# Even and odd columns in a triangular substitution, its reordering on ScalarE, and the first query weights of the last stage in places of their own

## The chip, the cores and the metric

One core of one Trainium2 chip runs the whole program in one launch. The metric is the time of an execution on the device, in microseconds (us); the kernel before has a median of 973.35 over three runs (969.14 to 974.21). The engines are TensorE (PE in the profile, PEld its weight loads), VectorE (DVE), ScalarE (ACT), GpSimd (POOL) and SyncE (SP), which issues the weights' DMAs.

## The reference, cut to what matters

The model has four mixers on 256 tokens of width 1,024: latent attention, block attention with a relative bias, a gated delta rule, and an attention with a forget gate ("fox"). The first two have a feed-forward layer behind each. The change touches the third mixer and the start of the fourth. In the delta rule, chunks of 64 tokens need the solution of a unit lower triangular system for each head:

```
a_mat = jnp.where(strict, einsum('bhncd,bhnsd->bhncs', kb, kc) * decay, 0.0)
rhs   = jnp.concatenate([vc * bc[..., None], kb * jnp.exp(gcum)[..., None]], axis=-1)
sol   = lax.linalg.triangular_solve(a_mat, rhs, left_side=True, lower=True, unit_diagonal=True)
...
y = gdn_mixer(rms_norm_2(h, pre), ...);  h = h + rms_norm_2(y, gdn_post_norm)
...
q, z = split(rms_norm_2(h, fox_pre_norm) @ fox_w_in);  k, v, f = split(rms_norm_2(h, kv_norm) @ kv_w)
```

All is computed in float32.

## The kernel before, in words

A weight matrix comes in pieces of 128 x 1,024 through a ring of four buffers `raw` (`load_w`, L148). ScalarE rounds a piece to `whi` (L164), a second engine computes the rest `wlo` as raw minus `whi` (L165; this is called a split here), and three matmuls (L171 to L173) make the product: high by high, low by high, and high by the low part of the other side. `whi` and `wlo` have rings of four buffers too, so a new piece waits until TensorE has used an old one. `raw` is free when its split is done, and only then does SyncE issue the next DMA. The split runs on VectorE, unless `engines` says otherwise.

The order on each engine is set by a scheduler that goes by data dependencies, program order and its own reckoning of time. `queued(after)` (L140) adds that an instruction isn't issued ahead of a given one on its engine.

In the delta rule (`gdn`) the inverse is built from blocks of 32 x 32: 8 heads and 8 blocks of 32 tokens make 64 systems. `system` writes them to DRAM and reads them so that each of the 128 partitions has one system and half of the 32 right-hand columns (`bt`, `xb`): partitions 0 to 63 columns 0 to 15, the others 16 to 31. `substitute(j)` (L976, 31 steps, on POOL) makes one product (L978) and one subtraction (L980) over the rows below j and the columns that can be other than zero at step j, at most 16. All partitions run the same shape, so the columns of both halves count. `spread` (L986) writes the result to DRAM (`x_d`, two DMAs, L988) and reads it into the block diagonal of `X` (four DMAs, L992). `spread_T` (L999) transposes `X` on TensorE, ScalarE evacuates (L1000), and `grow` doubles the blocks from 32 to 128 (L1036, L1051). Beside the substitution TensorE computes the convolutions of queries and values, and the second half of the gate (`gate(1)`, evacuated by L842).

At the end of the third mixer `post_norm_out` (L767) runs `out_proj` for both row tiles t of 128 tokens. For each tile ScalarE sums squares (L775), VectorE multiplies by the gain (L776), takes a root in instructions on one column (L192 to L198) and adds to `x` (L783). The last stage (`fox`, L1159) begins with the first query weights (`wq0`, four pieces with splits on POOL). For each tile it transposes `x` (L1170), evacuates to two pairs `hTq` and `hTk` (L256 on ScalarE the high part, L257 on VectorE the low part), and multiplies `hTq` with `wq0` at once, 24 matmuls a tile. `qkv_quad` follows with the key weights, whose pieces come next in the same `raw` ring.

Of the kernel before, what the change touches and what calls it, by code (L numbers as in the profile page):

```python
# [58 lines left out]
def layout(inputs):  # L59
# [38 lines left out]
    for p in range(P):  # L98
        for c in range(16):
            eye[p, 16 * (p // 64) + c, c] = 1.0  # L100
# [10 lines left out]
def kernel(ctx: ExitStack, tc: tile.TileContext, I: dict, out: bass.AP, small_at: dict):  # L111
# [35 lines left out]

    def load_w(src, a, b, engines=None, into=None, after=None):  # L148
# [3 lines left out]
        for a0 in range(0, a, m):  # L152
# [10 lines left out]
            with queued(after):  # L163
                A.activation(hi[:, :k * b], rs, AF.Copy)  # L164
                e.tensor_tensor(lo[:, :k * b], rs, hi[:, :k * b].bitcast(F32), op=ALU.subtract)  # L165
# [600 lines left out]
    def post_norm_out(oT, w, gname, after, between=None):  # L766
# [6 lines left out]
        def then(t, hf, a):  # L773
            j = w2k([P, 512])
            A.activation(j, a, AF.Square, accum_out=ss[:, t, hf:hf + 1])  # L775
            V.tensor_tensor(yg[:, t, hf * 512:(hf + 1) * 512], a, gb[:, hf * 512:(hf + 1) * 512], op=ALU.mult)  # L776
            if hf == 1:
# [3 lines left out]
                for h2 in range(2):  # L781
                    c = slice(h2 * 512, (h2 + 1) * 512)
                    V.scalar_tensor_tensor(x[:, t, c], yg[:, t, c], r, x[:, t, c], op0=ALU.mult, op1=ALU.add)  # L783
                    after(t, h2)

        out_proj(oT, w, then, between)

# [21 lines left out]
    def gdn():  # L809
# [87 lines left out]

        def conv(part, hp):
# [15 lines left out]
            A.activation(dst, y, AF.Silu)  # L914
# [60 lines left out]
        def substitute(j):  # L975

            c, n = min(j + 1, 16), 31 - j
# [44 lines left out]
        def values(hp, vT):  # L1022
# [132 lines left out]
        post_norm_out(oT, wview("gdn_w_out_2", 0), "gdn_post_norm_2", lambda t, h2: None,  # L1155
# [3 lines left out]
    def fox():  # L1159
# [4 lines left out]
        wq0 = load_w(wz[:, :, 0:512], KD, 512, (G,))  # L1164
# [104 lines left out]
    gdn()  # L1269
    fox()  # L1270
# [24 lines left out]
```

## Time and profile before

| what | value |
|---|---|
| median of three runs | 973.35 us (969.14 to 974.21) |
| the profiled execution, its own time and its span | 977.16 us, 975.4 us |
| busy share: PE, PEld, DVE, ACT, POOL | 93%, 81%, 65%, 53%, 17% |
| delta rule: TensorE's last matmul beside the substitution ends | 736.2 us |
| its next work, the transposes of `X` | 756.40 us |
| first load of `wq0` issued by SyncE | 804.78 us |
| last matmul of `out_proj` ends | 817.2 us |
| TensorE busy from 850 to 950 us | 99.5 of 100 us |

The first three lines are the runs, the page's head and its table; the others are read from the timeline and the windows. A busy share is a mean over stages with different limits, so the wait that matters is to be looked for where TensorE has none of its work: the page's strip has its two deep dips near 745 and 825 us.

### The profile page before, as it was taken

How to read it: one execution, taken by the hardware profiler on the slowest of the kernel's cores; microseconds unless marked ns; L12 is line 12 of the kernel's file. 1: busy time of each engine (PE TensorE's matmuls, PEld its weight loads, DVE VectorE, ACT ScalarE, POOL GpSimd, SP SyncE). 2: the span in 40 equal slices, each digit the busy share in tenths (PEclk: the TensorE clock that was granted, in tenths of full speed). 3: DMA queues.
4: the chain of work that ended last, by engine and by line, in shares of the span. 5: the costliest groups of instructions: out<-in, count | busy, mean ns of one | idle time of the engine just before them, and what ended most of it. 6: DMA issues, size and time to landing. Idle time of an engine off the chain costs nothing.

```text
span 975.4 us, 14708 instructions
## 1 busy us (share of the span) xinstructions
PE 906.4 (93%) x5474; PEld 787.9 (81%) x5474; DVE 637.7 (65%) x1331; ACT 521.1 (53%) x963; POOL 167.1 (17%) x198
## 2 busy tenths in 40 slices
PE   8799889999999999999999999999991997999996
PEld 8576579988898787778999999889991985789884
DVE  6897366655555666757545655679981678767775
ACT  6675355544446555646534544478651134765653
POOL 1421122222222300022000000010497203000000
PEclk9899999999999999999999999999996898999998
DMA  8346137676666865436565666354743004365431
GB/s 290 113 153 189 51 118 215 193 208 192 194 205 197 164 215 153 152 108 196 193 211 178 197 203 185 85 167 150 194 163 87 22 23 153 117 208 178 145 109 66
DMA packets 97113, 154.62 MB, mean 159 GB/s; under 512 B 10649, under 2 KB 65729, under 8 KB 96785
## 3 DMA queue, kind: packets, MB, share of 16 engines
q1 hardware_dynamic: 87072, 141.53, 46.2%
q0 software_dynamic: 9824, 12.11, 6.0%
q8 instruction: 43, 0.70, 0.3%
q14 instruction: 30, 0.24, 0.1%
q10 hardware_dynamic: 144, 0.03, 0.0%
HBM read 147.84 MB, written 5.78 MB: 158 GB/s over the span
## 4 chain that ended last, share of the span: by engine, by line
PE 55%; DMA 13%; DVE 12%; ACT 9%; POOL 6%; issue 4%; DVEq 0%; ACTq 0%; SPq 0%; POOLq 0%
PE acc L171 12%; PE acc L173 11%; PE acc L172 11%; DMA raw<-in_mlp_w_in_dram 6%; PE aux L173 3%; PE aux L171 3%; PE aux L172 3%; DVE wlo L165 3%; ACT whi L164 3%; DMA bias_d<-s 2%; POOL s L980 2%; POOL s L978 2%; DVE s L165 1%; PE aux L1051 1%; DMA raw<-in_moba_w_qkv_dram 1%
## 5 line engine op out<-in xcount | busy, mean ns | idle before, releaser
L165 DVE TENSOR_TENSOR wlo<-raw,whi 128x1024 fp32r<-128x1024 f32 (+3 forms) x194 | 235.5, 1217 | 186.5 <-ACT whi L164 185.3
L164 ACT ACTIVATE whi<-raw 128x1024 fp32r<-128x1024 f32 (+3 forms) x206 | 210.5, 1026 | 212.5 <-DMA raw<-in_mlp_w_in_dram 136.2
L171 PE MATMUL acc<-whi,s 128*128 128x512 f32 (+2 forms) x424 | 170.3, 405 | 4.1 <-ACT whi L164 2.1
L172 PE MATMUL acc<-wlo,s 128*128 128x512 f32 (+2 forms) x424 | 166.9, 394 | 0.6 <-DVE wlo L165 0.4
L173 PE MATMUL acc<-whi,s 128*128 128x512 f32 (+2 forms) x424 | 165.2, 391 | 0.0
L173 PE MATMUL aux<-s,wlo 128*128 128x256 f32 (+2 forms) x528 | 149.5, 283 | 3.1 <-DVE wlo L165 3.1
L171 PE MATMUL aux<-s,whi 128*128 128x256 f32 (+2 forms) x528 | 149.4, 283 | 2.3 <-DVE s L257 2.3
L172 PE MATMUL aux<-s,whi 128*128 128x256 f32 (+2 forms) x528 | 149.3, 283 | 0.0
L171 PEld LDWEIGHTS aux<-s,whi 128*128 128x128 f32 (+2 forms) x528 | 99.6, 189 | 5.0 <-DVE s L257 2.8
L173 PEld LDWEIGHTS aux<-s,wlo 128*128 128x128 f32 (+2 forms) x528 | 99.6, 189 | 4.2 <-DVE wlo L165 3.5
L173 PE MATMUL acc<-s,w2k 128*128 128x512 f32 x256 | 100.5, 393 | 2.0 <-DVE w2k L674 2.0
L171 PE MATMUL acc<-s,w2k 128*128 128x512 f32 x256 | 100.3, 392 | 2.2 <-ACT w2k L673 2.2
L172 PEld LDWEIGHTS aux<-s,whi 128*128 128x128 f32 (+2 forms) x528 | 99.6, 189 | 1.6
L172 PE MATMUL acc<-s,w2k 128*128 128x512 f32 x256 | 100.0, 391 | 0.0
L171 PEld LDWEIGHTS acc<-whi,s 128*128 128x128 f32 x424 | 80.8, 191 | 23.6 <-ACT whi L164 3.0
L173 PEld LDWEIGHTS acc<-whi,s 128*128 128x128 f32 x424 | 81.0, 191 | 15.5 <-DVE s L257 0.7
L172 PEld LDWEIGHTS acc<-wlo,s 128*128 128x128 f32 x424 | 81.0, 191 | 14.2 <-DVE wlo L165 1.4
L165 DVE TENSOR_TENSOR s<-raw,s 128x1024 fp32r<-128x1024 f32 x60 | 70.8, 1219 | 7.3 <-ACT s L164 7.3
L173 PE MATMUL acc<-s,wlo 128*128 128x256 f32 x256 | 72.8, 285 | 1.1 <-DVE wlo L165 1.1
L172 PE MATMUL acc<-s,whi 128*128 128x256 f32 x256 | 73.0, 285 | 0.5 <-DVE s L257 0.2
L171 PE MATMUL acc<-s,whi 128*128 128x256 f32 x256 | 73.0, 285 | 0.4 <-ACT s L256 0.2
L423 POOL DMA_DIRECT2D bias_d<-s x64 | 47.2, 825 | 142.7 <-ACT s L417 123.3
(350 smaller groups left out, 1496.9 us busy)
## 6 DMA issues: line engine op xcount, KB each, us to landing
raw<-in_mlp_w_in_dram SPq DMA_DIRECT2D x64, 512.0 KB, 5.2
raw<-in_mlp_w_out_dram SPq DMA_DIRECT2D x64, 512.0 KB, 4.0
raw<-in_gdn_w_in_dram SPq DMA_DIRECT2D x32, 512.0 KB, 4.2
raw<-in_moba_w_qkv_dram SPq DMA_DIRECT2D x24, 512.0 KB, 4.6
raw<-in_fox_w_in_dram SPq DMA_DIRECT2D x16, 512.0 KB, 4.8
raw<-in_kv_w_dram SPq DMA_DIRECT2D x16, 512.0 KB, 3.9
raw<-in_mla_w_o_dram SPq DMA_DIRECT2D x8, 512.0 KB, 4.0
bias_d<-s POOLq DMA_DIRECT2D x64, 64.0 KB, 4.7
```

The lines of the kernel that those rows point to most:

```text
L164: A.activation(hi[:, :k * b], rs, AF.Copy)
L165: e.tensor_tensor(lo[:, :k * b], rs, hi[:, :k * b].bitcast(F32), op=ALU.subtract)
L171: T.matmul(o, lhsT=l[0], rhs=r[0], start=start, stop=False)
L172: T.matmul(o, lhsT=l[0], rhs=r[1], start=False, stop=False)
L173: T.matmul(o, lhsT=l[1], rhs=r[0], start=False, stop=stop)
L423: nc.gpsimd.dma_start(bias_d[q0:q0 + 8].rearrange("g h k -> h g k"), stg[r0:r0 + 8], accum_op=ALU.add if part else ALU.bypass)
L978: G.tensor_tensor(t3[:, 0:n, 0:c], xb[:, j, 0:c][:, None, :].to_broadcast([P, n, c]), bt[:, j, j + 1:32][:, :, None].to_broadcast([P, n, c ...
L980: G.tensor_tensor(xb[:, j + 1:32, 0:c], xb[:, j + 1:32, 0:c], t3[:, 0:n, 0:c], op=ALU.subtract)
L1051: T.matmul(px[z][:, j * P:(j + 1) * P], lhsT=a, rhs=b, start=True, stop=True)
```

## The change

**Substitution.** The two halves of a system's columns are now the even and the odd ones (`eye`), so at step j there are j//2+1 columns to do on either half, and no longer min(j+1, 16). `x_d` has a place for each half, so that a partition writes 512 numbers in one row; the four reads go to a staging tile `stg` (in the room of `bt`), and four copies on ScalarE (`place`) put the even and odd columns side by side in `X`. They are queued behind the last convolution's Silu and the last split that was traced before.

**Last stage.** The four pieces of `wq0` have tiles of their own (in the rooms of `X`, `aT`, `kt` and `S1`, which are free by then), their splits run on VectorE, and pieces 2 to 4 are queued behind what `post_norm_out` returns for row tile 0: its second addition to `x` on VectorE, and its last sum of squares on ScalarE.

```diff
-            eye[p, 16 * (p // 64) + c, c] = 1.0
+            eye[p, 2 * c + p // 64, c] = 1.0
...
             with queued(after):
-                A.activation(hi[:, :k * b], rs, AF.Copy)
-                e.tensor_tensor(lo[:, :k * b], rs, hi[:, :k * b].bitcast(F32), op=ALU.subtract)
+                i = A.activation(hi[:, :k * b], rs, AF.Copy)
+                j = e.tensor_tensor(lo[:, :k * b], rs, hi[:, :k * b].bitcast(F32), op=ALU.subtract)
+            split[:] = [i.ins, j.ins]
...
-            A.activation(j, a, AF.Square, accum_out=ss[:, t, hf:hf + 1])
+            sq = [A.activation(j, a, AF.Square, accum_out=ss[:, t, hf:hf + 1]).ins]
...
-                    V.scalar_tensor_tensor(x[:, t, c], yg[:, t, c], r, x[:, t, c], op0=ALU.mult, op1=ALU.add)
+                    i = V.scalar_tensor_tensor(x[:, t, c], yg[:, t, c], r, x[:, t, c], op0=ALU.mult, op1=ALU.add)
                     after(t, h2)
+                rows[t] = [i.ins, sq[0]]
...
-            c, n = min(j + 1, 16), 31 - j
+            c, n = j // 2 + 1, 31 - j
...
-            x_d = dr.tile([4, 16, 32, 32], F32, tag="x_d", name="x_d")
-            for ch in range(2):
-                nc.gpsimd.dma_start(x_d[:, :, :, 16 * ch:16 * ch + 16].rearrange("b u i c -> (b u) i c"),
-                                  xb[64 * ch:64 * ch + 64])
+            x_d = dr.tile([4, 2, 16, 32, 16], F32, tag="x_d", name="x_d")
+            for h in range(2):
+                nc.gpsimd.dma_start(x_d[:, h], xb[64 * h:64 * h + 64])
+            stg = inv[:, 0:512].rearrange("p (h u c) -> p h u c", h=2, u=16)
             for b in range(4):
                 bs = slice(32 * b, 32 * b + 32)
-                last = nc.gpsimd.dma_start(X[bs, 0, :, bs], x_d[b].rearrange("u i c -> i u c"))
-            return last
+                last = nc.gpsimd.dma_start(stg[bs], x_d[b].rearrange("h u i c -> i (h u) c"))
+            return stg, last
+
+        def place(stg):
+            for b in range(4):
+                bs = slice(32 * b, 32 * b + 32)
+                o = X[bs, 0, :, bs].rearrange("p u (c h) -> p h u c", h=2)
+                A.activation(o, stg[bs], AF.Copy)
...
-        last = spread()
+        stg, last = spread()
         f, i, y = pend.pop(0)
         gate(1, hT, None, lambda: f(i, y))
+        with queued(behind + split):
+            place(stg)
         spread_T()
...
-        wq0 = load_w(wz[:, :, 0:512], KD, 512, (G,))
+        w8 = slot(8, [P, 2, 2048], F32R)
+        wl = (slot(13, [P, 2048], F32R), slot(14, [P, 2048], F32R))
+        wq0 = []
+        for c in range(4):
+            h2 = slice(1024 * (c % 2), 1024 * (c % 2) + 1024)
+            wq0 += load_w(wz[:, 2 * c:2 * c + 2, 0:512], 2, 512, into=(w8[:, c // 2, h2], wl[c // 2][:, h2]),
+                          after=rows[0] if c else None)
```

Line numbers of the new file are 2 to 26 higher than those of the kernel before; the rows of the order below have each file's own. On POOL, the end of the substitution and the spread (`s_6328` holds `bt`, `xb` and the staging tile, `s_6329` is `X`), before:

```order
L978 TENSOR_TENSOR s_6328<-s_6328 128x48
L980 TENSOR_TENSOR s_6328<-s_6328 128x48
L978 TENSOR_TENSOR s_6328<-s_6328 128x32
L980 TENSOR_TENSOR s_6328<-s_6328 128x32
L978 TENSOR_TENSOR s_6328<-s_6328 128x16
L980 TENSOR_TENSOR s_6328<-s_6328 128x16
L988 DMA x_d<-s_6328 2048x1x16 x2
L992 DMA s_6329<-x_d 32x16x32 x4
L1084 TENSOR_TENSOR s_6319<-s_6319,s_6293 128x8x128
```

and now:

```order
L986 TENSOR_TENSOR s_6328<-s_6328 128x3x15
L988 TENSOR_TENSOR s_6328<-s_6328 128x3x15
L986 TENSOR_TENSOR s_6328<-s_6328 128x2x15
L988 TENSOR_TENSOR s_6328<-s_6328 128x2x15
L986 TENSOR_TENSOR s_6328<-s_6328 128x16
L988 TENSOR_TENSOR s_6328<-s_6328 128x16
L997 DMA x_d<-s_6328 4x16x512 x2
L1001 DMA s_6328<-x_d 32x32x16 x4
L1102 TENSOR_TENSOR s_6319<-s_6319,s_6293 128x8x128
```

The last steps have half the columns or fewer, the writes to `x_d` have other rows, and the reads go to the staging tile with twice as many rows of half the length.

On ScalarE, the place of the four copies (L1008 in the new file; `s_6127` is the gate, L914 and L922 the last Silu), before:

```order
L842 ACTIVATE s_6127<-acc 128x512
L914 ACTIVATE w2k<-w2k 128x512
L164 ACTIVATE whi<-raw 128x1024
L842 ACTIVATE s_6127<-acc 128x512
L1000 ACTIVATE s_6329<-aux 128x512 x4
L164 ACTIVATE whi<-raw 128x1024
L1122 ACTIVATE s_6322<-aux 128x512 x2
```

and now:

```order
L848 ACTIVATE s_6127<-acc 128x512
L922 ACTIVATE w2k<-w2k 128x512
L1008 ACTIVATE s_6329<-s_6328 32x2x16x16 x4
L848 ACTIVATE s_6127<-acc 128x512
L166 ACTIVATE whi<-raw 128x1024
L1015 ACTIVATE s_6329<-aux 128x512 x4
L166 ACTIVATE whi<-raw 128x1024
L1140 ACTIVATE s_6322<-aux 128x512 x2
```

One split's rounding and the second evacuation of the gate have changed places with the copies: they now stand behind them, and ahead of the evacuations of the transposes.

On VectorE, from the end of the root for row tile 0 into the start of the last stage (`s_7917`/`s_7921` are products with the gain, `s_8125`/`s_8129` the low part of `hTq`), before:

```order
L198 SCALAR_TENSOR_TENSOR prr<-pe,prr 128x1
L197 SCALAR_TENSOR_TENSOR pe<-prr,pe 128x1
L198 SCALAR_TENSOR_TENSOR prr<-pe,prr 128x1
L783 SCALAR_TENSOR_TENSOR x<-s_7917,prr,x 128x512 x2
L776 TENSOR_TENSOR s_7917<-acc,s_7914 128x512 x2
L192 TENSOR_SCALAR pe<-pss 128x1
L193 TENSOR_SCALAR rq_i<-pe 128x1
L194 TENSOR_SCALAR pe<-pe 128x1
L195 TENSOR_SCALAR prr<-rq_i 128x1
L257 SCALAR_TENSOR_TENSOR s_8125<-aux,gains,s_8124 128x128
L197 SCALAR_TENSOR_TENSOR pe<-prr,pe 128x1
L257 SCALAR_TENSOR_TENSOR s_8125<-aux,gains,s_8124 128x128
```

and now:

```order
L200 SCALAR_TENSOR_TENSOR pe<-prr,pe 128x1
L201 SCALAR_TENSOR_TENSOR prr<-pe,prr 128x1
L786 SCALAR_TENSOR_TENSOR x<-s_7921,prr,x 128x512 x2
L167 TENSOR_TENSOR s_8131<-raw,s_8130 128x1024
L779 TENSOR_TENSOR s_7921<-acc,s_7918 128x512 x2
L195 TENSOR_SCALAR pe<-pss 128x1
L167 TENSOR_TENSOR s_8132<-raw,s_8130 128x1024
L196 TENSOR_SCALAR rq_i<-pe 128x1
L197 TENSOR_SCALAR pe<-pe 128x1
L167 TENSOR_TENSOR s_8132<-raw,s_8130 128x1024
L198 TENSOR_SCALAR prr<-rq_i 128x1
L260 SCALAR_TENSOR_TENSOR s_8129<-aux,gains,s_8128 128x128
```

Three of the four splits of `wq0` (the rows that write `s_8131` and `s_8132`) have come in between; the first stands ahead of the products for tile 0. On ScalarE, at the same place (`s_8130` is the high part of `wq0`, `s_8128` the high part of `hTq`, `s_8126` that of `hTk`), before:

```order
L164 ACTIVATE whi<-raw 128x1024 x4
L775 ACTIVATE w2k,pss<-acc 128x512 x2
L164 ACTIVATE whi<-raw 128x1024 x3
L775 ACTIVATE w2k,pss<-acc 128x512 x2
L164 ACTIVATE whi<-raw 128x1024
L256 ACTIVATE s_8124<-aux,gains 128x128 x8
L256 ACTIVATE s_8122<-aux,gains 128x128 x5
L708 ACTIVATE s_8414<-acc 128x512
```

and now:

```order
L166 ACTIVATE whi<-raw 128x1024 x4
L166 ACTIVATE s_8130<-raw 128x1024
L778 ACTIVATE w2k,pss<-acc 128x512 x2
L166 ACTIVATE s_8130<-raw 128x1024 x3
L166 ACTIVATE whi<-raw 128x64
L778 ACTIVATE w2k,pss<-acc 128x512 x2
L259 ACTIVATE s_8128<-aux,gains 128x128 x2
L166 ACTIVATE whi<-raw 128x1024
L259 ACTIVATE s_8128<-aux,gains 128x128 x5
L166 ACTIVATE whi<-raw 128x1024
L259 ACTIVATE s_8128<-aux,gains 128x128
L259 ACTIVATE s_8126<-aux,gains 128x128
```

The roundings of `wq0` are behind the squares of tile 0, and those of the key weights (`whi`) have come in between the evacuations of `hTq` and `hTk`.

## Rows read from the trace of the kernel before

**Rows 1.** Timeline of TensorE: start, us, engine, line, op, tiles, [idle before, releaser].
```profile
756.40 3.65 PE L999 MATMUL aux<-gains,s 128*128 128x128 f32 x16 [20.60 <-DMA s<-x_d]
...
824.38 1.97 PE L1170 MATMUL aux<-gains,x 128*128 128x128 f32 x8 [7.01 <-DVE x L783]
...
827.03 0.76 PE L173 MATMUL acc<-whi,s 128*128 128x512 f32 x1
...
833.18 1.04 PE L1170 MATMUL aux<-gains,x 128*128 128x128 f32 x8
```

**Rows 2.** Timeline of POOL, 690 to 755 us, same columns.
```profile
690.96 1.08 POOL L970 DMA_DIRECT2D s<-n_d  x2 [2.30 <-DMA n_d<-s]
...
698.07 0.24 POOL L978 TENSOR_TENSOR s<-s 128x31 f32<-128x31 f32 x1 [6.03 <-DMA s<-n_d]
...
721.90 0.75 POOL L980 TENSOR_TENSOR s<-s 128x255 f32<-128x255 f32 x1
...
722.73 0.62 POOL L978 TENSOR_TENSOR s<-s 128x256 f32<-128x256 f32 x1
...
723.43 1.76 POOL L980 TENSOR_TENSOR s<-s 128x256 f32<-128x256 f32 x1
...
743.80 0.22 POOL L980 TENSOR_TENSOR s<-s 128x16 f32<-128x16 f32 x1
...
745.17 2.22 POOL L988 DMA_DIRECT2D x_d<-s  x2 [1.15 <-issue]
...
751.73 2.58 POOL L992 DMA_DIRECT2D s<-x_d  x4 [4.34 <-DMA x_d<-s]
```

**Rows 3.** Groups by line, 697 to 745 us: count, busy us, mean ns, idle before.
```profile
L980 POOL TENSOR_TENSOR s<-s 128x112 f32<-128x112 f32 (+27 forms) x31 | 22.0, 710 | 2.4
...
L978 POOL TENSOR_TENSOR s<-s 128x112 f32<-128x112 f32 (+27 forms) x31 | 19.2, 618 | 8.4 <-DMA s<-n_d 6.0
...
L165 DVE TENSOR_TENSOR wlo<-raw,whi 128x1024 fp32r<-128x1024 f32 x12 | 15.7, 1308 | 2.6 <-ACT whi L164 2.6
```

**Rows 4.** Timeline of VectorE, the eleventh split beside the substitution.
```profile
731.03 1.27 DVE L165 TENSOR_TENSOR wlo<-raw,whi 128x1024 fp32r<-128x1024 f32 x1
```

**Rows 5.** DMA issues: tiles, queue, count, KB each, median us to landing.
```profile
x_d<-s POOLq DMA_DIRECT2D x2, 128.0 KB, 4.8
...
s<-x_d POOLq DMA_DIRECT2D x4, 64.0 KB, 2.4
...
s<-in_eye_dram POOLq DMA_DIRECT2D x1, 256.0 KB, 3.0
```

**Rows 6.** Timeline of ScalarE, one copy from SBUF to SBUF.
```profile
725.07 0.63 ACT L914 ACTIVATE w2k<-w2k 128x512 f32<-128x512 f32 x1 [0.30 <-DVE w2k L911]
```

**Rows 7.** Timeline of VectorE and POOL, 812 to 831 us.
```profile
812.00 1.37 DVE L776 TENSOR_TENSOR s<-acc,s 128x512 f32<-128x512 f32 x2 [3.11 <-ACT w2k L775]
...
814.35 0.22 DVE L197 SCALAR_TENSOR_TENSOR pe<-prr,pe 128x1 f32<-128x1 f32 x1
...
814.47 9.31 POOL L165 TENSOR_TENSOR wlo<-raw,whi 128x1024 fp32r<-128x1024 f32 x4 [20.39 <-ACT whi L164]
...
814.61 2.28 DVE L198 SCALAR_TENSOR_TENSOR prr<-pe,prr 128x1 f32<-128x1 f32 x1
...
821.53 3.46 DVE L783 SCALAR_TENSOR_TENSOR x<-s,prr,x 128x512 f32<-128x512 f32 x2
...
829.21 1.41 DVE L783 SCALAR_TENSOR_TENSOR x<-s,prr,x 128x512 f32<-128x512 f32 x2
```

**Rows 8.** DMA issues of the last stage's first weights, same columns.
```profile
raw<-in_fox_w_in_dram SPq DMA_DIRECT2D x4, 512.0 KB, 5.6
...
raw<-in_kv_w_dram SPq DMA_DIRECT2D x8, 512.0 KB, 4.0
```

**Rows 9.** Windows: stretch, length, busy us of each engine, TensorE's granted clock, DMA.
```profile
821.00:822.00 1.00, 0.00 (x0) 0.00 (x0) 0.96 (x2) 0.00 (x0) 1.00 (x2) 1.00 0.96 369
...
822.00:823.00 1.00, 0.00 (x0) 0.00 (x0) 1.00 (x1) 0.00 (x0) 1.00 (x1) 0.76 0.58 109
```

More of the change, by code (lines that the diff above doesn't have):

```diff
@@ L146, in queued @@
             yield
+    split = []
     def load_w(src, a, b, engines=None, into=None, after=None):
@@ L782, in then @@
                     c = slice(h2 * 512, (h2 + 1) * 512)
-                    V.scalar_tensor_tensor(x[:, t, c], yg[:, t, c], r, x[:, t, c], op0=ALU.mult, op1=ALU.add)
+                    i = V.scalar_tensor_tensor(x[:, t, c], yg[:, t, c], r, x[:, t, c], op0=ALU.mult, op1=ALU.add)
                     after(t, h2)
+                rows[t] = [i.ins, sq[0]]
+        rows = {}
         out_proj(oT, w, then, between)
+        return rows
     def softplus_neg(dst, u_in, n):
@@ L896, in gdn @@
         vt = slot(7, [P, NT, H, P])
+        behind = []
         def conv(part, hp):
@@ L913, in conv @@
             dst = (qT, kT)[part][:, 2 * hp:2 * hp + 2, :] if part < 2 else w2k([P, 2, S])
-            A.activation(dst, y, AF.Silu)
+            behind[0:1] = [A.activation(dst, y, AF.Silu).ins]
             return dst
@@ L1028, in values @@
             for t in range(NT):
-                V.tensor_tensor(vt[:, t, hs], p[:, 256 * t:256 * t + 256].rearrange("p (a b) -> p a b", a=2),
-                                rki[:, t, hs, None].to_broadcast([P, 2, P]), op=ALU.mult)
+                i = V.tensor_tensor(vt[:, t, hs], p[:, 256 * t:256 * t + 256].rearrange("p (a b) -> p a b", a=2),
+                                    rki[:, t, hs, None].to_broadcast([P, 2, P]), op=ALU.mult)
+            behind[1:] = [i.ins]
         def grow_a(s, u4):
@@ L1154, in gdn, with fox @@
         out_quad_T(0, 1)
-        post_norm_out(oT, wview("gdn_w_out_2", 0), "gdn_post_norm_2", lambda t, h2: None,
+        return post_norm_out(oT, wview("gdn_w_out_2", 0), "gdn_post_norm_2", lambda t, h2: None,
                       lambda: [out_quad_T(1, q4) for q4 in range(2)])
-    def fox():
+    def fox(rows):
         hTk, hTq = pair_tile(1, KD), pair_tile(11, KD)
@@ L1268 @@
     mlp(1)
-    gdn()
-    fox()
+    fox(gdn())
 _INS = ["x", "mla_w_in", "mla_w_uq", "mla_w_ukv", "mla_w_o", "moba_w_qkv", "moba_w_o", "mlp_w_in", "mlp_w_out",
```

## The prediction, made before the changed kernel was timed

> **What bounds the kernel now.** I read the page's busy table first (TensorE busy for 93% of the span), then its strip of 40 slices, which dips in two places, then TensorE's part of the timeline there. Two waits stand out [rows 1]: 20.60 us before the transposes of L999, which needed the DMA that fills `X`, and 7.01 us before L1170, which needed `x` from VectorE (L783). Behind the second, TensorE hardly rests until its last work (the windows in the section on the profile), so whatever either wait loses is lost from the end too. Everything before 733 us stands in the same order in both kernels.
>
> The POOL timeline shows what fills the first wait [rows 2]. The substitution is a chain of 62 instructions from 698.07 to 744.02, and behind it come two DMAs from 745.17, four from 751.73, and TensorE at 756.40. TensorE ran out of other work at 736.2 (the table of the profile), so the chain is late by all of the wait, and a microsecond taken from it is one gained.
>
> **First part, the substitution.** Clean instructions give a line: 16 elements take 0.22 us (subtraction), 256 take 0.62 (product, L978), 255 take 0.75 (subtraction, L980) [rows 2]. That is about 0.19 each plus 0.0039 per element of a pair of product and subtraction. Summed over the 31 steps, rows left times columns is 4,776 before and 2,856 now (columns j//2+1 in place of min(j+1, 16)). Clean time is thus 11.8 + 18.6 = 30.4 us before. The rows add up to 22.0 + 19.2 = 41.2 [rows 3], so 10.8 us are something else. In the same stretch VectorE ran exactly 12 splits L165 [rows 3], and 12 POOL instructions are too long by 0.85 to 1.09 us each, such as the L980 of 1.76 us at 723.43, beside a clean 0.75 [rows 2]. I price a split that meets the chain at 0.9.
>
> Now: 11.8 + 11.1 = 22.9, the same 61 gaps (45.95 − 41.2 = 4.8), and 0.9 for each split that still falls inside. The eleventh starts at 731.03 [rows 4], so eleven do: 9.9. The end is 698.07 + 37.6 = 735.7, which is 8.3 us earlier. The number of instructions and the splits don't shrink, so halving the work doesn't halve the chain. Bounds: no split met (27.7, end 725.8) and twelve met plus no gain from shorter rows (end as now).
>
> **The spread.** The wait of 1.15 us ahead of it stays: 736.85. The two writes had 2,048 pieces of 64 B and took 1.11 us each to issue; with 64 rows of 2 KB each I take 0.54, as the two loads at 690.96 with as many rows [rows 2]. The second is issued at 737.4. Landing: 4.8 as now is the upper end, 2.4 (the small DMAs) the lower, and I take the 3.0 of the load with rows of 2 KB [rows 5]: 740.4. Then 0.55 as now, and four reads that now move 1,024 pieces of 64 B in place of 512 of 128 B. Issue took 0.65 for 512 pieces and 1.11 for 2,048 [rows 2], so 0.81 by a straight line; the last is issued at 743.4. Landing lies between 2.4 and 4.8 [rows 5]; nearer to the DMA of the same size, I take 2.9: 746.3.
>
> New are four copies on ScalarE (L1008 of the new file) that scatter the columns. A copy of 512 elements from SBUF took 0.63 [rows 6]; three lie under the later reads and the last is on the path: 0.65, and 0.2 to TensorE, as now. TensorE starts at 747.15 in place of 756.40: **9.2 us earlier**. If all four copies came behind the last landing, 1.9 would go; with the lower ends 1.6 would be added to the gain, and with both landings at 4.8 and all issues at 1.11, 5.2 would go. The writes of a strided row are not in the trace; twice the copy's time would cost 0.6.
>
> One rule speaks against this part. The Trainium skill, "DMA: Bandwidth & Descriptors", section on why a DMA increments its semaphore by 16, says a DMA uses the largest number of engines up to 16 that divides the slowest dimension of both sides. The new write is listed as 4x16x512, so it would run on 4 engines, the old one (2048x1x16) on 16. Rows don't show such a DMA; from the page's 27 GB/s per engine, 32 KB each would take some 0.9 us more (an estimate), and the sum would be 8.3.
>
> On ScalarE the copies stand ahead of the gate's second L842 and of one split of w_out, which now wait until 747. Neither is needed soon: L842 frees an accumulator that out_proj takes some 25 us later, and that split feeds out_proj. Both do stand ahead of the first L1000; but the transposes run at low clock there, then as now, and set the pace of the four evacuations, so I charge nothing (half a microsecond if not). That the split leaves its old place also takes the twelfth split out of the chain.
>
> **Second part, the last stage.** Before, four splits of 1,024 columns ran on POOL from 814.47 for 9.31 us [rows 7]. Beside them, VectorE's instructions on one column took 2.28 us (0.22 just before), and the two L783 3.46 in place of 1.41. This is the path: L783 gives `x` to the transposes L1170. Without POOL the three slow instructions before L783 take 0.7 in place of 6.9 (814.61 to 821.53), and the pair 1.4.
>
> The SBUF page of the Trainium skill ("SBUF — State Buffer", section "Who interferes with whom") says that a DVE instruction with two SBUF inputs and a reading GpSimd instruction lock each other out whole. The rows agree, with 2.28 beside 2.3, and by that rule all of it goes, as I reckon.
>
> What comes instead are four splits of 1.23 in VectorE's order: one ahead of L776 for row tile 0, one behind L783, two inside the root for tile 1. On VectorE's clock of before: the first needs weights that are issued at 804.78 (the table of the profile) and land 5.6 later [rows 8], so ScalarE is done at 811.5, the split at 812.7, and L776 starts there and not at 812.00 [rows 7]. L776 twice 1.3, root 2.0, L783 1.4: 817.4. The transposes no longer wait, for TensorE is in tile 1 of out_proj until 817.2; they end near 818.4. VectorE: split 818.6, L776 819.9, 0.24, split 821.3, 0.2, split 822.6, 0.1, first L257 at 823.0. TensorE's first L173 needs that L257: 823.05 in place of 827.03 [rows 1], **4.0 us earlier**.
>
> The clock gives more. It was full until 822 and low from 822.5 on [rows 9]; L1170 then took 1.97 where the next one took 1.04 [rows 1]. Now TensorE rests from 819.0 to 823.0, about as long as the first row shows it resting at full clock. I take full clock: the 24 matmuls of tile 0 end at 828.4 (the third pair waits for its left side: ScalarE meets the first key weights, issued at 818.6, landing 4.0 later [rows 8], split by 823.9). The second L1170 starts there, not at 833.18: 4.8 earlier. After that the rings `whi` and `wlo` are free for key weights while the query matmuls run, and in the new order 15 key matmuls (3.4 us) lie between those of tile 1, where before TensorE waited for `hTq`. I put the whole part at **5.5 us**, between 2 (low clock, and each of the three weight loads seen by ScalarE 0.7 late) and 7.5. The four splits add 4.9 us to VectorE, which was busy for three quarters of that stage.
>
> **Sum.** 9.2 + 5.5 = 14.7. The profiled execution took 977.16 us, 1.8 around its span of 975.4, so a profile of the new kernel should have a span near 961. The median of the runs, 973.35, is 3.8 below that execution; the same subtraction gives **958.5 us**.
>
> **Rivals.**
> - Only the spread gains. VectorE's four splits stand where TensorE waits, and the low clock stays: the second part gives 0 to 2, 962 to 964. Against it: 6.2 + 2.0 us of mutual blocking go for sure, and 4.9 come.
> - Only the last stage gains much. Both landings and issues at their upper ends, the copies bunched: the first part gives 2 to 4, 964 to 966. For it: 1,024 pieces where 512 were. Against it: the issue's straight line.
> - More than forecast, 950 to 953: few splits meet the shorter chain, since POOL instructions are shorter, and TensorE finds the feed ready in tile 1.
> - Slower, 975 or more: ScalarE's place for the key weights. Three L164 now stand between the evacuations of `hTq`, and each waits for a load whose buffer is free only behind a split. At 4.0 per landing the waits overlap. If they ran one after another, each would cost 4.0 + 1.06 + 1.2, near 19 us for three, and the 14.7 would be gone; it decides from about 5 us per load that TensorE sees. The buffers, however, come free at 818.6, 821.3 and 822.6, ahead of any evacuation, so only a landing of over 9 us would do it.
> - No change: a chain that is off the path. Against it: 20.60 us of TensorE waiting for it alone.
>
> **How the numbers follow.** Forecast 0.70 (its own range 953 to 964), only the spread 0.12, only the last stage 0.07, more 0.06, no change 0.03, slower 0.02. The range that leaves out no more than 2 in 10 is **951 to 967**. What a measurement of this kernel can tell from no change is about 0.5% (4.9 us): faster by more 0.92, within 0.05, slower 0.03.
>
> **What would show it.** In the profile of the changed kernel: L978 and L980 of old at about 33 us busy with eleven long ones; TensorE's wait for the fill of `X` near 11 us, for ScalarE's copies by name; no POOL work on splits; VectorE's one-column instructions all under 0.3; TensorE's rest behind out_proj near 4 us and, at its end, the granted clock full. The forecast is wrong if the chain ends after 740, if landing takes over 4 us, if the clock falls there all the same, or if ScalarE waits for loads among L256.

## The result, and the profile of the changed kernel

The changed kernel has a median of 967.24 us over 20 runs (963.36 to 972.53), the kernel before one of 975.43 over 20 runs (969.14 to 977.96): ratio 0.9924, 95% interval 0.9910 to 0.9939. It is faster by some 8 us; forecast were 14.7, and 958.5 in a range that ended at 967.0. The profiled execution took 965.93, 1.8 around its span of 964.1.

The spans differ by 11.3, but 3.3 of that is not the change's. TensorE's rest before the transposes of `X` began at 735.80 before (756.40 less 20.60 [rows 1]; the 736.2 of the table of the profile is 0.4 late) and begins at 732.52 now, with the same work ahead of it; in the other profiles below it begins between 729.9 and 739.1. I therefore count from there: 239.6 us to the end before, 231.6 now, **8.0 less**.

TensorE's timeline, with the work that answers to [rows 1] (start, us, engine, line, op, tiles, [idle before, and what ended it]):

```profile
743.78 3.68 PE L1014 MATMUL aux<-gains,s 128*128 128x128 f32 x16 [11.26 <-ACT s L1008]
...
805.10 1.04 PE L1196 MATMUL aux<-gains,x 128*128 128x128 f32 x8
...
809.78 0.50 PE L176 MATMUL acc<-s,s 128*128 128x512 f32 x1 [2.75 <-DVE s L260]
...
810.95 0.80 PE L174 MATMUL acc<-s,s 128*128 128x512 f32 x1 [0.67 <-ACT s L259]
...
817.33 1.03 PE L1196 MATMUL aux<-gains,x 128*128 128x128 f32 x8
...
870.82 0.38 PE L176 MATMUL acc<-s,wlo 128*128 128x256 f32 x1 [3.67 <-DVE wlo L167]
```

The wait of 20.60 is now 11.26, and the 7.01 before the transposes of `x` are gone. But there are waits that weren't there: 3.4 us in row tile 0 of the last stage, and 3.67 us at the first gate weights, 50 us later. The stretches between these marks, in us (TensorE has the same number of matmuls in each of the last three in both kernels):

| stretch | before | now | change |
|---|---|---|---|
| TensorE's rest before the transposes of `X` | 20.60 | 11.26 | −9.34 |
| from there to the transposes of `x`, tile 0 | 67.98 | 61.32 | −6.66 |
| from there to those of tile 1 | 8.80 | 12.23 | +3.43 |
| from there to the end | 142.22 | 146.77 | +4.55 |

Half of what was won is given back in the last two. The first of them is the order on VectorE and ScalarE at the start of the stage (same columns):

```profile
806.93 1.22 DVE L167 TENSOR_TENSOR s<-raw,s 128x1024 fp32r<-128x1024 f32 x1
...
808.19 1.22 DVE L167 TENSOR_TENSOR s<-raw,s 128x1024 fp32r<-128x1024 f32 x1
...
809.39 0.34 DVE L260 SCALAR_TENSOR_TENSOR s<-aux,gains,s 128x128 fp32r<-128x128 f32 x1
```
```profile
809.58 1.06 ACT L166 ACTIVATE whi<-raw 128x1024 fp32r<-128x1024 f32 x1 [3.04 <-DMA raw<-in_kv_w_dram]
810.55 0.61 ACT L259 ACTIVATE s<-aux,gains 128x128 fp32r<-128x128 f32 x2
```

`x` is in time, but the first low part of `hTq` (L260) stands behind two splits, and the third high part (L259) behind a key weight that ScalarE waits 3.04 us for. Then TensorE's granted clock falls to half from 810.7 to 814.1, as the windows show (stretch, its length, busy us of PE, PEld, DVE, ACT, POOL, then TensorE's granted clock, DMA share, GB/s):

```profile
809.00:810.00 1.00, 0.22 (x1) 0.19 (x1) 1.00 (x5) 0.42 (x1) 0.00 (x0) 1.00 0.47 59
810.00:811.00 1.00, 0.33 (x2) 0.05 (x1) 0.26 (x3) 1.00 (x3) 0.00 (x0) 0.87 0.96 369
811.00:812.00 1.00, 1.00 (x3) 0.81 (x4) 1.00 (x6) 0.82 (x3) 0.00 (x0) 0.50 1.07 264
...
814.00:815.00 1.00, 1.00 (x5) 0.77 (x5) 1.00 (x5) 0.94 (x1) 0.00 (x0) 0.92 0.00 0
```

The second loss is the forget gate's decay. Its cumulated logarithms (`cr`) go to DRAM and come back on all partitions (`cr_d`, two DMAs on POOL's queue); 16 instructions on VectorE (L1244) make the bias of all eight heads in one block, and the next split of gate weights stands behind it. POOL's rows, VectorE's, and the two DMAs (KB each, us to landing):

```profile
852.77 0.55 POOL L1238 DMA_DIRECT2D cr_d<-w1k  x1 [70.81 <-ACT w1k L1236]
858.34 0.57 POOL L1240 DMA_DIRECT2D s<-cr_d  x1 [5.01 <-DMA cr_d<-w1k]
```
```profile
863.67 5.36 DVE L1244 SCALAR_TENSOR_TENSOR s<-s,cc,small 128x128 f32<-128x128 f32 x16 [3.47 <-DMA s<-cr_d]
868.95 0.69 DVE L1264 TENSOR_TENSOR w2k<-acc,w1k 128x512 f32<-128x512 f32 x1
869.54 3.49 DVE L167 TENSOR_TENSOR wlo<-raw,whi 128x1024 fp32r<-128x1024 f32 x3
```
```profile
s<-cr_d POOLq DMA_DIRECT2D x1, 1024.0 KB, 5.2
cr_d<-w1k POOLq DMA_DIRECT2D x1, 8.0 KB, 5.0
```

The first of those splits ends at 870.76, and TensorE goes on. The same rows of the kernel before (VectorE, then TensorE) had no wait, but hardly any room:

```profile
874.00 5.36 DVE L1218 SCALAR_TENSOR_TENSOR s<-s,cc,small 128x128 f32<-128x128 f32 x16 [1.08 <-DMA s<-cr_d]
...
879.88 1.21 DVE L165 TENSOR_TENSOR wlo<-raw,whi 128x1024 fp32r<-128x1024 f32 x1
```
```profile
881.76 0.28 PE L173 MATMUL acc<-s,wlo 128*128 128x256 f32 x1
```

That split was done at 881.09, 0.67 us before TensorE took it up. At the transposes of tile 1 TensorE is now 15.85 us earlier than before (817.33, 833.18), the block's end only 10.3 (869.03, 879.36): the write to `cr_d` was issued 35.4 behind these transposes in place of 33.0, and took 5.0 to land in place of 2.3. What TensorE wins beyond that chain it loses waiting for it.

### The profile page after: what moved, and what is told of

It is laid out like the page before. It is cut to its first block, busy times and chain, and to the rows that moved or that the text cites. A ratio compares the mean times of both kernels' runs of the same rounds, so it can differ in the third digit from the quotient of the medians.

```text
span 964.1 us, 14699 instructions
## 1 busy us (share of the span) xinstructions
PE 905.0 (94%) x5474; PEld 789.9 (82%) x5474; DVE 635.4 (66%) x1335; ACT 522.7 (54%) x967; POOL 151.1 (16%) x194
## 5 line engine op out<-in xcount | busy, mean ns | idle before, releaser
L166 ACT ACTIVATE whi<-raw 128x1024 fp32r<-128x1024 f32 (+3 forms) x202 | 206.0, 1025 | 217.0 <-DMA raw<-in_mlp_w_in_dram 137.6
L174 PE MATMUL acc<-whi,s 128*128 128x512 f32 (+2 forms) x408 | 162.1, 401 | 3.5 <-ACT whi L166 2.6
L175 PE MATMUL acc<-wlo,s 128*128 128x512 f32 (+2 forms) x408 | 160.4, 394 | 0.5 <-DVE wlo L167 0.5
L176 PE MATMUL acc<-whi,s 128*128 128x512 f32 (+2 forms) x408 | 158.9, 391 | 0.0
L176 PE MATMUL aux<-s,wlo 128*128 128x256 f32 (+2 forms) x528 | 149.5, 283 | 3.1 <-DVE wlo L167 3.1
L176 PEld LDWEIGHTS aux<-s,wlo 128*128 128x128 f32 (+2 forms) x528 | 99.6, 189 | 3.9 <-DVE wlo L167 3.6
L176 PE MATMUL acc<-s,w2k 128*128 128x512 f32 x256 | 100.2, 391 | 1.1 <-DVE w2k L677 1.1
L174 PEld LDWEIGHTS acc<-whi,s 128*128 128x128 f32 x408 | 77.6, 191 | 20.6 <-ACT whi L166 3.1
L176 PEld LDWEIGHTS acc<-whi,s 128*128 128x128 f32 x408 | 78.6, 193 | 14.0 <-DVE s L1278 0.3
L175 PEld LDWEIGHTS acc<-wlo,s 128*128 128x128 f32 x408 | 78.2, 192 | 13.2 <-DVE wlo L167 1.3
L167 DVE TENSOR_TENSOR s<-raw,s 128x1024 fp32r<-128x1024 f32 x64 | 75.7, 1219 | 5.3 <-ACT s L166 5.3
L176 PE MATMUL acc<-s,wlo 128*128 128x256 f32 x256 | 73.4, 288 | 6.2 <-DVE wlo L167 6.2
L166 ACT ACTIVATE s<-raw 128x1024 fp32r<-128x1024 f32 x68 | 68.3, 1048 | 7.2 <-DMA raw<-in_mlp_w_out_dram 6.0
```

The costliest lines, as they stand in the source:

```text
L166: i = A.activation(hi[:, :k * b], rs, AF.Copy)
L167: j = e.tensor_tensor(lo[:, :k * b], rs, hi[:, :k * b].bitcast(F32), op=ALU.subtract)
L174: T.matmul(o, lhsT=l[0], rhs=r[0], start=start, stop=False)
L175: T.matmul(o, lhsT=l[0], rhs=r[1], start=False, stop=False)
L176: T.matmul(o, lhsT=l[1], rhs=r[0], start=False, stop=stop)
```

## The experiments

One table for all (us; the four stretches as above, then the landing of the decay's write and read, and TensorE's wait at the gate weights). The ratio is to the kernel before on the same chip, with its 95% interval. The stretches come from one profile of each kernel: the median less the sum of its four stretches runs from 732.6 to 737.1 over these kernels, so a difference of a few us in stretches alone shows little.

| kernel | median | ratio | rest before `X` | to tile 0 | to tile 1 | to the end | landings | gate wait |
|---|---|---|---|---|---|---|---|---|
| before | 975.43 | | 20.60 | 67.98 | 8.80 | 142.22 | 2.3, 5.1 | 0 |
| changed | 967.24 | 0.9924 (0.9910 to 0.9939) | 11.26 | 61.32 | 12.23 | 146.77 | 5.0, 5.2 | 3.67 |
| 1 delta rule only | 967.81 | 0.9905 (0.9871 to 0.9938) | 12.12 | 68.49 | 9.08 | 142.15 | 2.5, 5.1 | 0 |
| 2 last stage only | 976.40 | 1.0008 (0.9984 to 1.0032) | 20.45 | 61.14 | 12.24 | 147.81 | 5.4, 5.0 | 3.88 |
| 3 decay by heads | 964.14 | 0.9882 (0.9854 to 0.9910) | 12.28 | 60.60 | 13.28 | 140.91 | 5.1, 5.2 | 0 |
| 4 splits on POOL | 968.88 | 0.9932 (0.9911 to 0.9952) | 12.18 | 65.78 | 8.72 | 147.90 | 2.8, 8.1 | 3.72 |
| 5 delta rule, decay by heads | 965.93 | 0.9917 (0.9884 to 0.9951) | 12.41 | 68.61 | 9.14 | 142.47 | 1.7, 7.2 | 0 |
| 6 other order, decay by heads | 959.71 | 0.9836 (0.9803 to 0.9869) | 12.40 | 62.08 | 9.30 | 141.25 | 3.8, 5.1 | 0 |
| 7 ring, decay by heads | 961.45 | 0.9859 (0.9825 to 0.9892) | 13.34 | 62.14 | 11.29 | 142.13 | 2.1, 4.9 | 0 |
| 8 rows of `x_d` | 965.42 | one run | 9.79 | 60.97 | 13.47 | 146.49 | 4.6, 5.5 | 3.53 |
| 9 = 6 and 8 | 957.33 | 0.9830 (0.9799 to 0.9861) | 10.57 | 60.81 | 9.30 | 141.24 | 3.9, 5.0 | 0 |
| 10 ring | 964.19 | 0.9898 (0.9877 to 0.9919) | 13.10 | 62.17 | 11.30 | 142.18 | 1.8, 5.6 | 0 |
| 11 write on ScalarE's queue | 965.32 | 0.9913 (0.9882 to 0.9944) | 12.38 | 60.62 | 13.36 | 142.32 | at most 3.1, 5.0 | 0.35 |
| 12 own places, no order | 970.06 | 0.9947 (0.9925 to 0.9970) | 12.15 | 70.91 | 4.39 | 145.52 | 1.7, 5.2 | 0 |

In runs 4 and 12 some matmuls of tile 0 come behind the first transpose of tile 1 (4 and 18 of 24), so their last two stretches are to be read as a sum.

**1, 2: each part alone.** Run 1 has the last stage as before, by the edit shown; run 2 has the delta rule as before (`eye`, `substitute` and `spread` as they were, no `place`):

```diff
-        wq0 = []  ... load_w(..., into=(...), after=rows[0] if c else None)
+        wq0 = load_w(wz[:, :, 0:512], KD, 512, (G,))
```

> The changed kernel with its last stage as before (the four splits of the first query weights back on POOL, in the ring); only the delta rule is changed. Theory A: this part alone gives its 9.3 us (TensorE waits 11.3 in place of 20.6 before the transposes of X), since all that comes behind, the decay's round trip through DRAM too, moves with it: 965 to 967, ratio 0.990 to 0.992, as fast as both parts together or faster, and no wait of over 1 us at the first gate weights. Rival B: half of this part is lost behind it (bunched copies, four evacuations late): 968 to 970, ratio 0.994, and the last stage's part brings the rest. Rival C (my forecast's sum): 966, and both parts together would then have to stand 5 lower, which they don't.

> Only the last stage is changed; substitution and spread as before. Theory A: TensorE starts the last stage's matmuls 3 to 5 us earlier, and gives it back at the first gate weights, whose split stands behind the 16 decay instructions on VectorE, and these behind the broadcast of the decay from DRAM; a new wait of 2 to 4 us there and low clock behind it; time 973 to 977, ratio 0.998 to 1.002. Rival B: the gain of this part arrives: 969 to 971, ratio 0.994 to 0.996, no such wait.

Theory A holds for both. In run 1 no wait stands at the first gate weights and the ratio is in A's range; its median of 967.81 is 0.8 above it and just short of B's. The delta rule's part is all that the changed kernel has: 0.9905 beside 0.9924. The last stage's part alone changes nothing (1.0008), though it reaches the transposes of `x` 6.8 us sooner; its timeline of TensorE has the wait again, on the old delta rule:

```profile
881.54 0.58 PE L176 MATMUL acc<-s,wlo 128*128 128x256 f32 x1 [3.88 <-DVE wlo L167]
```

**3: the decay by heads.** The two instructions of a head are traced ahead of that head's attention:

```diff
-        for h in range(H):
+        def decay(h):
             for t, (a0, b0) in enumerate(((0, 128), (128, 384))):
                 V.scalar_tensor_tensor(db[:, h, a0:b0], ...)
...
                 h = 4 * g4 + j
+                decay(h)
                 o = attend(...)
```

> The changed kernel, with the 16 decay instructions (5.4 us of VectorE) traced head by head ahead of each head's attention, so that one split of the gate weights now stands ahead of the first of them on VectorE. Theory A: TensorE's wait of 3.67 us for that split goes, and the low clock behind it (872.1 to 875.4) too: 3.5 to 5.5 us faster than the changed kernel, 961.5 to 964, ratio to before 0.986 to 0.988. Rival B: the next split, behind nine decays, is late instead, and no more than 1 us is won (966 to 968). Rival C: the wait was an accident of the one profiled execution (a slow landing), and the time stays at 967.

964.14, ratio 0.9882: just above A's range, with A's mechanism. The write lands as late as before (5.1), VectorE waits for the read as before; but one split now stands ahead of the block, which is nine instructions long, and TensorE doesn't wait. VectorE's timeline:

```profile
864.39 1.22 DVE L167 TENSOR_TENSOR wlo<-raw,whi 128x1024 fp32r<-128x1024 f32 x1
...
867.98 2.99 DVE L1245 SCALAR_TENSOR_TENSOR s<-s,cc,small 128x128 f32<-128x128 f32 x9 [2.37 <-DMA s<-cr_d]
```

The last stretch takes 140.91 in place of 146.77. The ratio falls from 0.9924 to 0.9882, with intervals that just touch.

**4: the splits back on POOL,** in their own places (`engines=(G,)` added to the call).

> The changed kernel with the four splits of the first query weights on POOL as before, but in their own places and in the set order. Theory A: the one-column instructions of VectorE beside them are back at 2.3 us each and L786 at 3.4, and TensorE waits 6 to 7 us before the transposes of x in place of none; but the decay's chain has 3 to 5 us less to lose, so the time is only 0 to 3 us longer than with the changed kernel: 967 to 970, ratio 0.992 to 0.995. Rival B: all of the gain at the start of the last stage counts to the end: 970 to 973, ratio 0.996 to 0.998.

968.88, in A's range. TensorE's wait before the transposes of `x` is back, 4.85 rather than 6 to 7, and the ratio differs from the changed kernel's by 0.0008 only. The gate wait is there too, here because the read of 1 MB took 8.1.

**5: is the decay edit a gain by itself?** Run 1 with the edit of run 3.

> The delta rule's part alone (last stage as before) with the decay traced head by head. Theory A: without the last stage's part TensorE never waits at the first gate weights, so this edit alone wins nothing: 966 to 969, ratio 0.989 to 0.993; the 3 us that the same edit won on the changed kernel are then the last stage's part, set free. Rival B: the edit is a gain by itself, whatever the start of the stage does: 963.5 to 965.5, ratio 0.987 to 0.989, and the last stage's part is worth nothing even without the cap.

No: the last stretch stays (142.47 beside 142.15), as theory A has it, and the ratio moves within its interval (0.9917 beside 0.9905); the median of 965.93 alone lies between A and B. What the edit won on the changed kernel is the last stage's part set free; runs 6 and 7, timed beside the same runs of the kernel before as run 5, have that part in other forms, and every run of theirs (956.64 to 963.88) is below every one of run 5 (965.17 to 970.30).

**6: another order at the start of the last stage,** with run 3's edit. Nothing is queued ahead of the second split; the third and fourth come behind the low parts of `hTq` k=3 and k=5, and later weights behind the eighth part:

```diff
-            with queued(after):
+            with queued(after or held):
...
+                    if t == 0 and gn == "fox_pre_norm_2" and k in (3, 5):
+                        o, raw, r = low.pop(0)
+                        with queued(last[1:]):
+                            V.tensor_tensor(o, raw, r.bitcast(F32), op=ALU.subtract)
+                    if t == 0 and gn == "fox_pre_norm_2" and k == KD - 1:
+                        held[:] = last
```

> The changed kernel with the decay head by head, and with another order at the start of the last stage: the second split of the first query weights ahead of L779 (not queued), the third and fourth on VectorE behind the low parts of hTq k=3 and k=5 of row tile 0, and every later rounding of weights on ScalarE behind the eighth. Theory A: the wait of 2.75 us (behind two splits of 1.22 us on VectorE) and that of 0.3 to 0.7 us (ScalarE waiting for a key weight's load ahead of hTq) fall to under 0.5 together, and without the pause the granted clock stays full there (11 matmuls at 0.43 us in place of 0.23 cost some 1.6 us): 2.5 to 4 us faster than with the decay edit alone (964.1): 960 to 961.5, ratio 0.984 to 0.986. Rival B: VectorE has no slack in that stretch, the splits only move, the second tile's transposes wait in place of the first's matmuls: 0 to 1 us, 963 to 964.

959.71: A, and a little more. From tile 0 to tile 1 it takes 9.30 in place of 12.2 to 13.4. TensorE's waits of 0.33, 0.46 and 0.53 are all that is left there, and the granted clock stays full, as the windows show where the changed kernel had 0.50 (first TensorE's longest wait in tile 0, then two windows):

```profile
811.02 0.50 PE L175 MATMUL acc<-s,s 128*128 128x512 f32 x1 [0.53 <-DVE s L1211]
```
```profile
810.00:811.00 1.00, 0.49 (x2) 0.05 (x1) 1.00 (x3) 0.11 (x1) 0.00 (x0) 1.00 0.24 59
811.00:812.00 1.00, 0.98 (x4) 0.85 (x5) 1.00 (x4) 0.67 (x3) 0.00 (x0) 1.00 0.82 291
```

**7, 10: only the engine.** The first query weights in the old ring, without an order, split on VectorE (`load_w(wz[:, :, 0:512], KD, 512)`); run 7 with the decay by heads, run 10 without.

> The kernel with the decay head by head (964.1), but the first query weights in the old ring and without a set order, their splits on VectorE: of the last stage's part only the engine is changed. Theory A: most of the gain is the engine's (no POOL split beside VectorE): TensorE waits 2 to 4 us at the start of the stage, and key weights can't come ahead of the query matmuls; 964 to 967, ratio 0.988 to 0.991. Rival B: places and order carry the gain: 967 to 969, ratio 0.991 to 0.993, as with the old splits on POOL.

> The changed kernel with the first query weights in the old ring and no set order, their splits on VectorE; the decay as in the changed kernel, 16 instructions in one block. With the decay head by head this form took 961.5, and its write of the decay landed in 2.1 us (5.0 in the changed kernel). Theory A: the loss of the changed kernel hangs on the places and the set order, which bring the decay's write right behind two weight loads; here it lands in 2 to 2.7, VectorE's block of 16 is done in time, TensorE waits under 1.5 us at the gate weights: 961 to 964, ratio 0.985 to 0.988. Rival B: any faster start of the last stage runs into the block of 16: a wait of 2.5 to 4 us as in the changed kernel, 965 to 967.

Run 7 beat both guesses (961.45). Run 10 lies just above A (964.19, ratio 0.9898), without a gate wait. With the decay by heads the engine alone carries the part: from run 5 to run 7 only the engine changes, and the median falls by 4.5 us. With the block of 16 (runs 1 and 10) the stretches say 3.1, but the ratios, 0.9905 and 0.9898, show no difference. Places and order add nothing that can be told (0.9882 with them, 0.9859 without); with the block of 16 they cost 2.8 by the stretches (0.9924 beside 0.9898, with intervals that overlap). In their order the write to `cr_d` is issued 0.5 us behind a weight load, in the ring's 2.5 us. Run 10's two DMAs:

```profile
s<-cr_d POOLq DMA_DIRECT2D x1, 1024.0 KB, 5.6
cr_d<-w1k POOLq DMA_DIRECT2D x1, 8.0 KB, 1.8
```

**8, 9: the shape of the write to `x_d`.** 64 rows of 512 numbers, read by eight DMAs; run 9 has it with run 6's edits.

```diff
-            x_d = dr.tile([4, 2, 16, 32, 16], F32, tag="x_d", name="x_d")
+            x_d = dr.tile([2, 4, 16, 32, 16], F32, tag="x_d", name="x_d")
-                nc.gpsimd.dma_start(x_d[:, h], xb[64 * h:64 * h + 64])
+                nc.gpsimd.dma_start(x_d[h].rearrange("b u i c -> (b u) (i c)"), xb[64 * h:64 * h + 64].rearrange("p i c -> p (i c)"))
-                last = nc.gpsimd.dma_start(stg[bs], x_d[b].rearrange("h u i c -> i (h u) c"))
+                for h in range(2):
+                    last = nc.gpsimd.dma_start(stg[bs, h], x_d[h, b].rearrange("u i c -> i u c"))
```

> The changed kernel with x_d laid out so that a write is 64 rows of 512 numbers (listed as 64x512 in place of 4x16x512); the reads are then eight of 32 KB. If a write's slowest dimension of 4 holds it to few engines (the rule weighed in the prediction), its landing falls from 3.7 to about 2.8 us. Rival: the landing stays at 3.5 to 3.9, since the number of rows and bytes is the same. The eight reads take 5 to 6.5 us to issue in place of 3.1, so TensorE starts 1 to 3 us later than in the changed kernel and the time says nothing on the rule.

> Both edits that helped put together: the other order at the start of the last stage with the decay head by head (959.7), and x_d in rows of 64x512 with eight reads (TensorE's wait 9.8 in place of 11.3 to 12.4). Theory A: the gains add, since both stand on TensorE's path: 1.5 to 2.6 us faster than without the rows, 957 to 958.5, ratio 0.980 to 0.983. Rival: the next bound (VectorE, contiguous in the first 10 us of the last stage, or the decay's broadcast) takes it: 959.5 to 960.5.

The landing falls from 3.7 to 2.4, and the reads start 1.42 us after the issue of the writes ends, in place of 4.70 (POOL's timeline, then the two groups of DMAs, of run 8):

```profile
732.15 1.12 POOL L997 DMA_DIRECT2D x_d<-s  x2 [0.30 <-POOL s L988]
734.69 1.33 POOL L1002 DMA_DIRECT2D s<-x_d  x2 [1.42 <-DMA x_d<-s]
```
```profile
x_d<-s POOLq DMA_DIRECT2D x2, 128.0 KB, 2.4
s<-x_d POOLq DMA_DIRECT2D x8, 32.0 KB, 2.2
```

Not all of that is the landing. A read now needs one write only: the first read goes out at 734.69, 0.28 behind the landing of the first write (734.41) and ahead of that of the second (735.24). The eight reads take 5.7 us to issue, as expected, but against what I expected they don't eat the gain up: from the end of the substitution to TensorE's start it is 10.8 us in runs 8 and 9, 12.3 to 12.7 in the others with the new spread. Run 9 has a median of 957.33, in A's range, and a ratio of 0.9830, run 6 one of 0.9836: by the stretches 3.1 us less than run 6, by the ratios no difference that can be told. Run 9 is faster than the changed kernel and the kernel before.

**11: the decay's write on ScalarE's queue** (`nc.scalar.dma_start(cr_d, cr)`).

> The changed kernel with the 8 KB write of the decay issued by ScalarE on its own DMA queue, in place of POOL; the read stays on POOL. Theory A: it lands late because two weight loads of 512 KB were issued 0.5 and 1.9 us before it and their pieces stand in the same 16 engines: landing 4 to 5 us, wait of 3 to 4 us at the gate weights, 966 to 968. Rival B: POOL's queue is late by itself: landing 2 to 2.6 us, the wait falls to about 1, 964 to 965.

In between. Weight loads were issued 0.2 and 1.7 us before it (0.5 and 1.9 in the changed kernel); it was issued at 853.25 and had landed by 856.37, when POOL could issue the read: at most 3.1 us, and the gate wait is 0.35 (ScalarE's, POOL's and TensorE's timelines):

```profile
853.25 0.53 ACTq L1238 DMA_DIRECT2D cr_d<-w1k  x1
```
```profile
856.37 0.55 POOL L1240 DMA_DIRECT2D s<-cr_d  x1 [74.77 <-DMA cr_d<-w1k]
```
```profile
868.58 0.39 PE L176 MATMUL acc<-s,wlo 128*128 128x256 f32 x1 [0.35 <-DVE wlo L167]
```

With loads as close ahead, the four profiles that write from POOL's queue have 4.6 to 5.4. This one profile points at POOL's queue in that traffic rather than at the traffic alone. The median gains less than the stretches (228.7 in place of 231.6): 0.9913 beside 0.9924, with intervals that overlap.

**12: own places without an order** (`after=None`).

> The changed kernel with the first query weights in their own places and split on VectorE, but without the set order (nothing is queued behind row tile 0). The scheduler then puts all four splits and three of later weights ahead of the second addition to x of row tile 0, some 8.6 us of VectorE. Theory A: the set order is what keeps L786 early once places of their own let weights run ahead: TensorE waits 4 to 7 us before the transposes of x, with low clock, and the time is 967 to 971, ratio 0.992 to 0.996, as with the splits on POOL or worse. Rival B: TensorE's later matmuls have their feed ready and make up for it: 963 to 966, ratio 0.987 to 0.990.

970.06: A. VectorE does seven splits of 1,024 columns before it adds to `x` of tile 0, and TensorE waits 10.06 us, longer than the 4 to 7 expected:

```profile
822.19 1.97 PE L1196 MATMUL aux<-gains,x 128*128 128x128 f32 x8 [10.06 <-DVE x L786]
```

The order is what places of their own need; with the ring it isn't needed.

## Why the prediction was wrong

**The substitution was right.** POOL's chain runs 37.74 us from 693.75 (forecast 37.6; before 45.95 [rows 3]), with exactly eleven instructions too long by 0.85 to 1.06. The groups that answer to [rows 3] (count, busy us, mean ns, idle before):

```profile
L986 POOL TENSOR_TENSOR s<-s 128x126 f32<-128x126 f32 (+22 forms) x31 | 17.1, 550 | 7.8 <-DMA s<-n_d 5.4
L988 POOL TENSOR_TENSOR s<-s 128x126 f32<-128x126 f32 (+22 forms) x31 | 15.9, 513 | 2.4
L167 DVE TENSOR_TENSOR wlo<-raw,whi 128x1024 fp32r<-128x1024 f32 x11 | 14.5, 1314 | 2.7 <-ACT whi L166 2.6
```

**The spread gave nothing;** forecast were 0.9. From the chain's end to TensorE it took 12.38 before and takes 12.29 now. The wait ahead of it was 0.30 in place of the 1.15 I kept, issues cost 0.66 (forecast 0.54) and 0.79 (0.81), the reads landed in 2.9 and the last copy alone lay on the path, both as taken. But the writes landed in 3.7, not 3.0 (the second, which is the one on the path, was issued at 732.48 and landed at 736.33), and from there to the first read at 737.80 it took 1.47, not 0.55. What fills the 1.47 the profile doesn't show ("issue").

```profile
731.79 1.31 POOL L997 DMA_DIRECT2D x_d<-s  x2 [0.30 <-POOL s L988]
737.80 3.14 POOL L1001 DMA_DIRECT2D s<-x_d  x4 [4.70 <-issue]
```
```profile
740.70 0.64 ACT L1008 ACTIVATE s<-s 32x512 f32<-32x512 f32 x1 [10.04 <-DMA s<-x_d]
741.54 2.19 ACT L1008 ACTIVATE s<-s 32x512 f32<-32x512 f32 x3 [0.20 <-DMA s<-x_d]
```

The landing is the place where I weighed the rule of the Trainium skill, "DMA: Bandwidth & Descriptors", section "Why a DMA increments its semaphore by 16 and not by 1", and went against it. By my estimate from the rule it would have been 3.9; run 8, where the write is listed as 64x512, shows 2.4. The traces agree with the rule: the DMA share was 0.36 while the two writes were under way (733.1 to 735.3) and 0.24, about 4 of 16 engines, with the second alone (735.4 to 735.9); in run 8 it was 0.74 over both (733.3 to 734.9). Run 8's writes also go to one stretch of DRAM each; no run has the one without the other. TensorE's rest is 9.3 shorter in this profile, but 1.0 of that is a chain that began 4.3 earlier where TensorE's rest began 3.3 earlier; that leaves 8.3, and the other profiles with this spread have 7.3 to 8.5. That is the rule's 8.3 and not my 9.2, in part by luck: the gap of 1.47 (0.55 taken) and the wait of 0.30 (1.15 taken) cancel.

**The start of the last stage was half right.** Without POOL's splits VectorE's instructions on one column are back at 0.14 to 0.22, and the two L786 at 1.41 [rows 7]. The first L176 comes 4.6 us sooner, counted from the transposes of `X` (66.0 in place of 70.6; forecast 4.0). But "I take full clock" failed: TensorE rested 2.75 and 0.67, and its clock was low from 810.7 to 814.1, some eight matmuls at 0.43 us in place of 0.23, or 1.6. Tile 1 comes 3.2 sooner, not 4.8. The 0.67 was in the sum in kind: there the third pair waits for the first key weights, at a price of some 0.3 (828.4 less 823.05 and 22 matmuls of 0.23). Their load was issued at 805.73 and landed in 3.8, near the 4.0 taken, so the rival about key weights, which has such loads one after another, didn't come. Run 6 shows that both waits were a matter of order.

**The step that failed** is "TensorE hardly rests until its last work, so whatever either wait loses is lost from the end too". No wait in 850 to 950 us did not mean that there was room. VectorE's block of 16 and the split behind it were 0.67 us ahead of TensorE; the decay's chain did not gain what TensorE gained, and the new wait of 3.67 us, with low clock behind it from 872 to 875.5 (16 matmuls at 0.21 in place of 0.12, or 1.5), took back the part's 3.2 and more. Runs 1, 2, 3 and 5 show it from all four sides: the first part alone has no such wait, the second alone has it (3.88) and gains nothing, the decay by heads takes it away, and without the second part that edit wins nothing. I had asked what is late next only up to the next matmul, not to the next point at which another chain joins TensorE's. Two of the signs I had named for a wrong forecast came, the fall of the clock and ScalarE's wait for a load among the L259; the loss that decided is in none of them.

**The base was off by 2.1.** I subtracted 3.8 from the profiled execution for a median over three runs; over 20 runs the kernel before has 975.43, and the subtraction would have been 1.7. In sum: 8 of 14.7 us. The second part, put at 5.5 because its blocking would "go for sure", did take the blocking away and gave nothing at the end as it was built. That is the outcome of the rival "only the spread gains", but not its reason: the low clock at the start of the stage took 1.6 of it, the block of the decay the rest.

## What to carry to other kernels

Where TensorE shows no wait over a stretch, look for the instruction of each other engine that releases it with the least room, and ask whether its chain moves with TensorE. Here it did when only the delta rule was changed (run 1), and did not when the last stage was: the DMA round trip in it was issued later and landed later. Long blocks of work that isn't needed yet, traced in one go ahead of weights, are worth cutting up before the stage ahead is made faster. And count from a mark that the change cannot touch: single spans of this kernel differ by several us in work that is the same.

## What the hardware showed that I had not expected

- The same 128 KB to DRAM landed in 3.7 us listed as 4x16x512, with a DMA share of 0.36 for two writes at once, and in 2.4 as 64x512, with 0.74, from the same queue.
- A write of 8 KB on POOL's queue landed in 1.7 to 2.5 us where the last load of 512 KB had been issued 2.5 us before it (five profiles), in 3.8 and 3.9 where it was 2.1, and in 4.6 to 5.4 where it was 0.5 (four profiles); runs 4 and 12 (0.8 and 2.8, 2.1 and 1.7) don't fit the row. From ScalarE's queue, 0.2 us behind such a load, it took at most 3.1 (one profile). Why POOL's queue should suffer more is open.
- A rest of 2.75 us and one of 0.67 behind it, 0.5 of work apart, ended with the clock low for 3.4 us (the same order: 3.4 in run 2, 6.8 in runs 3, 8 and 11). In runs 7 and 10 one rest of 2.5 over the same matmuls ended so too, low for 3.4. With waits of 0.70, 0.33, 0.46 and 0.53 us there (run 6) the clock stayed full.
